# Down stage: operand sets and weights asked for product by product on one queue; the second norm between up products; another order of the tail

## The chip, the cores and the metric

The kernel runs on one core of one Trainium2 chip. The metric is the device time of one execution in microseconds; a kernel is run several times and the median is compared. The core has five engines that each work through their own list of instructions in order: TensorE (PE; its weight loads are listed as PEld), VectorE (DVE), ScalarE (ACT), GpSimd (POOL) and SyncE (SP). They wait for each other by semaphores. DMA transfers are asked for by an instruction on one engine's list and then run beside the engines.

## The reference

The reference is one layer of a decoder trunk, applied to a prompt of 512 tokens and to 8 sequences of 4 new tokens, in float32, with D = 2048 and D_FF = 5504. What matters here is its second half:

```python
    h = h + jnp.concatenate([o_gla, o_nsa], axis=-1) @ w_out[i]
    f, conv_new = conv_ffn(rmsnorm(h, ffn_norm_g[i]), conv_s[i], ffn_w_up[i], ffn_conv_w[i],
                           ffn_conv_b[i], ffn_w_down[i])
    h = h + f
    h = h + jax.nn.sigmoid(h @ ple_w_gate[i] + ple_b_gate[i]) * (p[i] @ ple_w_proj[i])
...
y = rmsnorm(h, final_norm_g)
...
def conv_ffn(xn, prefix, w_up, conv_w, conv_b, w_down):
    a, u = jnp.split(xn @ w_up, 2, axis=-1)
    a_all = jnp.concatenate([prefix.astype(a.dtype), a], axis=1)
    c = a_all[:, 0:L] * conv_w[0] + a_all[:, 1:L + 1] * conv_w[1] + a_all[:, 2:L + 2] * conv_w[2] + conv_b
    h = jax.nn.gelu(c) * u
    return h @ w_down, a_all[:, -(CONV_W - 1):]
```

The outputs are y for both groups of tokens, the new cache rows, the new states, and the convolution's last rows.

## The kernel before

All 544 tokens stand along the free dimension, as two groups (G) of 272 columns (256 of the prompt, 16 new). Every operand of a product is split into a high part h, rounded to fp32r by ACT, and a low part l, the rest, formed by VectorE (`split`, lines L919 and L920; with a scale L1104 and L1105); a product of two numbers is h·h + h·l + l·h, so each 128 x 128 block of weights costs three matmuls. Weights come from memory by SP into a tile raw and are split into wh (ACT) and wl (VectorE).

The stages that matter, in order:

1. **w_out** (`half_out`): 16 blocks of rows, two PSUM banks (mp, mq). VectorE adds each into the residual (L1003); scaled residuals are split at once into the operands of up (a11, s1, s2, a12, s3). ACT squares each residual and VectorE adds it to acc2 (L1127). At the end `rms_bcast` turns acc2 into R2, one factor for each token: ones times acc2 on TensorE (L209, into the bank ob), a chain of small VectorE steps that end in rs_y (L211 to L216), a broadcast over the partitions on TensorE (L220, L222) and copies into R2 (L223 on ACT, L224 on VectorE). Since the norm is a factor of each token, up works on operands without it and applies R2 to its results (ae, L1242, and gl, L1258).
2. **Up**: 43 columns in the order `UP_ORDER`. Each column takes seven products (Strassen-Winograd) in place of eight: X with a11, Y with s1, X with s2, Z with a12, X with s3, Y with s4, X with a22, with 24 matmuls each (L1185). Weights are combined on VectorE between them (raw<-raw). The first two columns run together, product by product, so that the operands of s4 and a22 (`late_operands`) can be made meanwhile. A column ends with the convolution and the gelu, which leave one hidden tile uu; POOL stores the convolution's rows (cvo, L1246 to L1248). After every second column `pair_operands` forms the seven operands of the down stage, and SP stores them in memory (dd_a.., dd_s.., L1271; those of the last column, L1277).
3. **Down**: three phases over the hidden dimension (`PHASES`), each with four pairs of columns that run together (`together`); a column here yields two blocks of 128 outputs for each group. Again seven products a column, of 21 matmuls (24 for some in the last phase). The seven operand sets of a phase, da11, ds1, ds2, da12, ds3, ds4 and da22, are read back from memory in two pieces each by POOL's queue (L1324) into a staging tile sg, of which there are three, and split from there into h and l. The sets of the next phase replace those of the old one while the phase's last pair runs (`refill`). The results of a column are gathered in two tiles e (three buffers each) and added to the residual in memory by POOL's queue (rd<-e, L1367).
4. **Gates**: 16 blocks, each a full product, a sigmoid, and a multiplication by the projected input embedding (L1413 to L1422), with squares gathered in acc3.
5. **Tail**: the last two gates go group by group. After the second of them for one group `rms_bcast` makes R3 for that group, and every residual is multiplied by it (L1443), shared between VectorE and POOL by `YSEQ`, and stored by SP (L1444), two rows of blocks at a time.

The code is written in program order; a scheduler then sets the order of each engine's list from its own estimates, and `tc.issue_after(x)` forces an instruction behind x. Tiles come from pools, and a tile in a used place waits until its last reader is done.

## Time and profile before

| what | value |
|---|---|
| median of three runs | 2736.88 us (2735.01 to 2738.28) |
| the profiled execution | 2739.89 us |
| its span, first to last instruction | 2738.1 us |
| mean granted clock of TensorE | 0.986 |
| busy share of the span | PE 97%, PEld 95%, DVE 65%, ACT 42%, POOL 17% |

The profile is that of one execution. Its time contains the span and some 2 us around it. The granted clock is the share of TensorE's full speed (2.4 GHz) that it was given; 0.50 is the lower of its two levels. A row of a timeline gives start, length and what is computed from what; a number in brackets is the time for which the engine stood still before that instruction, with what released it. A length contains the overlap with the next instruction, so a series of equal instructions is better counted by their starts.

### The profile page before, as it was taken

The numbers are of one execution on the slowest core, as the hardware profiler recorded it, in microseconds if no ns is written. First come the engines' busy times: TensorE is split into PE (matmuls) and PEld (weight loads), VectorE is DVE, ScalarE is ACT, GpSimd is POOL, SyncE is SP. The second block draws the span as 40 slices with busy tenths as digits, with TensorE's granted clock in tenths as the row PEclk, the third lists the DMA queues.
The fourth block names the chain that finished last, engine by engine and source line by source line (L and its number), as shares of the span: only waits on it lengthen the run. The fifth ranks groups of instructions, "written<-read, shape, count | busy, mean of one in ns | idle before, by whom it ended". The sixth has DMA issues, their size and how long they took to land.

```text
span 2738.1 us, 51117 instructions
## 1 busy us (share of the span) xinstructions
PE 2654.1 (97%) x21258; PEld 2604.7 (95%) x21258; DVE 1776.0 (65%) x2545; ACT 1151.6 (42%) x1811; POOL 458.7 (17%) x617
## 2 busy tenths in 40 slices
PE   8999999999999999899999999999979999999996
PEld 7999999999999789899999999999979999999996
DVE  5323543322256677898888888888878777866434
ACT  4333433221135455454445444544445544544332
POOL 4531101101201200121112111211121111102001
PEclk9999999999999999999999999999989999999998
DMA  6432222332524824333433443334337565646332
GB/s 245 134 108 72 93 95 94 111 106 90 204 70 160 306 82 135 113 123 122 141 121 111 132 134 118 120 120 142 122 129 203 172 166 140 209 120 185 117 110 85
DMA packets 130217, 366.88 MB, mean 134 GB/s; under 512 B 16928, under 2 KB 42512, under 8 KB 126912
## 3 DMA queue, kind: packets, MB, share of 16 engines
q1 hardware_dynamic: 101840, 280.42, 31.0%
q0 software_dynamic: 28144, 83.18, 10.9%
q8 instruction: 167, 2.74, 0.4%
q14 instruction: 66, 0.54, 0.1%
HBM read 298.93 MB, written 64.61 MB: 133 GB/s over the span
## 4 chain that ended last, share of the span: by engine, by line
PE 80%; issue 8%; DMA 3%; DVE 2%; POOL 1%; ACT 1%; SPq 0%; DVEq 0%; POOLq 0%; ACTq 0%
PE mp L178 27%; PE X L1185 25%; PE Y L1185 12%; PE Z L1185 6%; PE mq L178 3%; PE sp L359 2%; DMA sg<-dd_a 1%; PE sp L996 1%; DMA KV<-in_cache_slc,idx 1%; POOL KV L338 1%; DMA sg<-dd_s 1%; PE so L616 0%; PE sp L956 0%; DVE resid L1443 0%; POOL rd L1367 0%
## 5 line engine op out<-in xcount | busy, mean ns | idle before, releaser
L919 ACT CAST wh<-raw 128x1024 fp32r<-128x1024 f32 (+1 forms) x397 | 405.3, 1031 | 487.6 <-PE X L1185 227.0
L920 DVE TENSOR_TENSOR wl<-raw,wh 128x1024 fp32r<-128x1024 f32 (+1 forms) x397 | 471.4, 1196 | 85.1 <-ACT wh L919 85.0
L168 ACT CAST wh<-raw 128x1024 fp32r<-128x1024 f32 (+2 forms) x175 | 171.9, 985 | 456.9 <-PE mp L178 405.8
L169 DVE TENSOR_TENSOR wl<-raw,wh 128x1024 fp32r<-128x1024 f32 (+2 forms) x175 | 200.0, 1145 | 221.2 <-ACT wh L168 217.4
L178 PE MATMUL mp<-xh,wh 128*128 128x272 f32 x1408 | 297.4, 291 | 2.5 <-DVE qk L465 2.5
L178 PE MATMUL mp<-xl,wh 128*128 128x272 f32 x1408 | 299.6, 292 | 0.0
L178 PE MATMUL mp<-xh,wl 128*128 128x272 f32 x1408 | 297.2, 292 | 0.8 <-DVE wl L169 0.8
L178 PEld LDWEIGHTS mp<-xh,wh 128*128 128x128 f32 x1408 | 223.5, 190 | 4.7 <-issue 2.7
L178 PEld LDWEIGHTS mp<-xl,wh 128*128 128x128 f32 x1408 | 223.8, 190 | 1.9 <-issue 0.7
L178 PEld LDWEIGHTS mp<-xh,wl 128*128 128x128 f32 x1408 | 223.4, 190 | 2.2 <-DVE wl L169 1.1
L1246 POOL COPY cvo<-ae 128x2 f32<-128x2 f32 x43 | 54.1, 1259 | 715.6 <-DVE ae L1242 715.6
L1185 PE MATMUL Y<-s,wh 128*128 128x272 f32 x688 | 131.8, 287 | 0.0
L1185 PE MATMUL X<-a,wh 128*128 128x272 f32 x688 | 131.2, 288 | 0.0
L1104 ACT ACTIVATE wh<-raw 128x896 fp32r<-128x896 f32 (+1 forms) x72 | 69.4, 965 | 99.3 <-PE X L1185 43.8
L1185 PEld LDWEIGHTS X<-a,wh 128*128 128x128 f32 x688 | 108.4, 189 | 0.0
L1185 PEld LDWEIGHTS Y<-s,wh 128*128 128x128 f32 x688 | 107.8, 188 | 0.0
L1105 DVE SCALAR_TENSOR_TENSOR wl<-raw,wh 128x896 fp32r<-128x896 f32 (+1 forms) x72 | 79.4, 1105 | 32.5 <-ACT wh L1104 32.4
L1185 PE MATMUL Z<-a12h,wh 128*128 128x272 f32 x344 | 99.9, 290 | 0.0
L1185 PE MATMUL X<-a11h,wh 128*128 128x272 f32 x344 | 99.9, 290 | 0.0
L1185 PE MATMUL X<-s2h,wh 128*128 128x272 f32 x344 | 99.6, 290 | 0.0
L1185 PE MATMUL X<-a11l,wh 128*128 128x272 f32 x344 | 99.5, 289 | 0.0
L1185 PE MATMUL X<-s3h,wh 128*128 128x272 f32 x344 | 99.4, 289 | 0.0
(524 smaller groups left out, 8078.3 us busy)
## 6 DMA issues: line engine op xcount, KB each, us to landing
raw<-in_w_up SPq DMA_DIRECT2D x172, 512.0 KB, 4.6
raw<-in_w_in SPq DMA_DIRECT2D x89, 512.0 KB, 3.6
raw<-in_w_db SPq DMA_DIRECT2D x48, 448.0 KB, 4.1
raw<-in_w_gate SPq DMA_DIRECT2D x32, 512.0 KB, 3.5
raw<-in_w_da SPq DMA_DIRECT2D x32, 448.0 KB, 3.9
rd<-e POOLq DMA_DIRECT2D x48, 272.0 KB, 4.5
raw<-in_w_out SPq DMA_DIRECT2D x24, 512.0 KB, 3.6
dd_s<-st SPq DMA_DIRECT2D x65, 136.0 KB, 5.0
```

The source lines that it names most:

```text
L168: nc.scalar.copy(wh[:, :m], raw[:, s:s + m])
L169: nc.vector.tensor_sub(wl[:, :m], raw[:, s:s + m], wh[:, :m].bitcast(F32))
L178: mm = nc.tensor.matmul(pp[g][:, :GN] if isinstance(pp, list) else pp[:, g, :GN], w, x[:, g], start=first, stop=last)
L338: nc.gpsimd.indirect_dma_start(out=out, out_offset=None, in_=I[cache], in_offset=bass.IndirectOffsetOnAxis(ap=idx[:, 4 * b + pg:4 * b + pg ...
L359: nc.tensor.matmul(at[j // 16], w1[j // 16][:, j % 16], rows[:, :, j % 16], start=j == 0, stop=j == 31, skip_group_check=True)
L919: nc.scalar.copy(hi, src)
L920: nc.vector.tensor_sub(lo, src, hi.bitcast(F32))
L996: nc.tensor.matmul(so, V[:, c, g * 128:g * 128 + 128], PT[:, c * 128:c * 128 + 128], start=False, stop=i == 1 and c == qt)
L1104: nc.scalar.activation(hl[0], src, AF.Copy, scale=scale)
L1105: nc.vector.scalar_tensor_tensor(hl[1], src, scale, hl[0].bitcast(F32), op0=ALU.mult, op1=ALU.subtract)
L1185: nc.tensor.matmul(ps[:, :GN], w[wi][:, k], a[k][xi], start=start and k == 0 and i == 0, stop=stop and k == n - 1 and i == 2, skip_group_c ...
L1246: nc.gpsimd.tensor_copy(cvo[:, 0:2], ae[:, 512:514])
```

## The change

The change has five parts, and the lists of instructions before and after show where each one lands.

**The norm of up.** `rms_bcast` becomes a generator (`rms_steps`) with a stop after the small VectorE chain and one after the broadcast. It no longer stands between w_out and up, but is one more member of `together` for the first two columns. The bank ob gets a pool of its own ahead of X, Y and Z, kept until the end of down; uu has three buffers in place of four.

TensorE's list at the end of w_out, before (onh and onl are the operands of w_out, mq its bank):

```order
L178 MATMUL mq<-onl_9384,wh 128x272 x2
L178 MATMUL mq<-onh_9383,wl 128x272 x2
L209 MATMUL ob<-ones,acc_10771 128x1 x5
L220 MATMUL ob<-cn,rs_y 128x128 x4
L222 MATMUL ob<-cn,rs_y 128x32
L1185 MATMUL X<-a11h_10688,wh 128x272
L1185 MATMUL X<-a11l_10689,wh 128x272
```

After, 24 rows of X<-a11 of the first column follow w_out's last row; this is where they end:

```order
L1193 MATMUL X<-a11l_10703,wh 128x272
L1193 MATMUL X<-a11h_10702,wl 128x272
L213 MATMUL ob<-ones,acc_10771 128x1 x5
L1193 MATMUL X<-a11h_10688,wh 128x272
L1193 MATMUL X<-a11l_10689,wh 128x272
L1193 MATMUL Y<-s1h_10704,wh 128x272
```

and, some 200 rows later, inside X<-s3:

```order
L1193 MATMUL X<-s3h_10762,wh 128x272
L1193 MATMUL X<-s3l_10763,wh 128x272
L225 MATMUL ob<-cn,rs_y 128x128 x4
L227 MATMUL ob<-cn,rs_y 128x32
L1193 MATMUL X<-s3h_10762,wl 128x272
L1193 MATMUL X<-s3h_10764,wh 128x272
```

The column sums (ob<-ones,acc) have moved behind the first column's X<-a11, and the broadcast (ob<-cn,rs_y) into X<-s3.

**The opening of down.** For the first pair of columns, sets and weights are asked for in the order of the products, all on SP's queue, each forced behind the one before (`in_order`): da11, a weight block for each of the two columns, ds1, two weight blocks, and so on. The staging tile sg is gone for all phases: a piece is loaded straight into the place of its l part, ACT rounds it into h, and VectorE replaces it by the difference.

SP's list at the end of up, before (raw<-in_w_da and raw<-in_w_db are weights of down):

```order
L1271 DMA dd_s_11749<-st 128x272
L1198 DMA raw<-in_w_da 128x896
L1271 DMA dd_s_11758<-st 128x272
L1198 DMA raw<-in_w_da 128x896
L1198 DMA raw<-in_w_db 128x896 x3
L1277 DMA dd_a_11743<-uu 128x272
L1277 DMA dd_s_11746<-uu 128x272
```

and after:

```order
L1279 DMA dd_s_11726<-st 128x272
L1279 DMA dd_s_11735<-st 128x272
L1360 DMA da11l<-dd_a_11718 128x1088
L1358 DMA da11l<-dd_a_11718 128x816
L1358 DMA raw<-in_w_da 128x896 x2
L1358 DMA ds1l<-dd_s_11721 128x1088
L1358 DMA ds1l<-dd_s_11721 128x816
L1358 DMA raw<-in_w_da 128x896 x2
L1358 DMA ds2l<-dd_s_11724 128x1088
L1358 DMA ds2l<-dd_s_11724 128x816
```

The loads of the sets, which stood on POOL's list behind the last out_conv, now stand on SP's, with the weights between them; the stores of the last column (L1277, now L1285) follow behind all of them.

VectorE's list at the first wl of Z, before (ds1l to da12l are l parts of sets; the last row is that wl, of the first column):

```order
L1105 SCALAR_TENSOR_TENSOR ds2l<-sg,ds2h 128x1088
L920 TENSOR_TENSOR wl<-raw,wh 128x896
L1105 SCALAR_TENSOR_TENSOR ds2l<-sg,ds2h 128x816
L1345 TENSOR_TENSOR raw<-raw 128x896
L920 TENSOR_TENSOR wl<-raw,wh 128x896
L920 TENSOR_TENSOR da12l<-sg,da12h 128x1088
L920 TENSOR_TENSOR wl<-raw,wh 128x896
L920 TENSOR_TENSOR da12l<-sg,da12h 128x816
L1105 SCALAR_TENSOR_TENSOR wl<-raw,wh 128x896
```

and after:

```order
L1283 TENSOR_TENSOR st<-uu 128x272
L1414 TENSOR_TENSOR raw<-raw 128x896
L1400 TENSOR_TENSOR raw<-raw 128x896
L926 TENSOR_TENSOR da12l<-da12l,da12h 128x1088
L926 TENSOR_TENSOR da12l<-da12l,da12h 128x816
L1400 TENSOR_TENSOR raw<-raw 128x896
L926 TENSOR_TENSOR wl<-raw,wh 128x896
L926 TENSOR_TENSOR ds3l<-ds3l,ds3h 128x1088
L926 TENSOR_TENSOR ds3l<-ds3l,ds3h 128x816
L926 TENSOR_TENSOR wl<-raw,wh 128x896
L1112 SCALAR_TENSOR_TENSOR wl<-raw,wh 128x896
```

Both pieces of ds3l, which followed that wl before, now stand ahead of the first wl of Z (the last row), and so do more of the additions raw<-raw. Ahead of these rows stand da11l, ds1l, ds2l and, of the last up column, ae, cc, gl and uu.

**Refills.** At a switch of phase the load of a set is still on POOL's list, but its target is the l part itself, so it waits until the set's last product is done. ACT's list at the first switch, before (e<-X and e<-Y are the copies of finished products of the new pair; wh in the order of the products X, X, Y, Y):

```order
L1365 COPY e_23770<-X 128x272
L919 CAST ds4h<-sg 128x816
L1365 COPY e_23809<-X 128x272
L919 CAST wh<-raw 128x896
L1337 COPY e_24242<-X 128x272
L919 CAST da22h<-sg 128x1088
L1337 COPY e_24281<-X 128x272
L919 CAST da22h<-sg 128x816
L919 CAST wh<-raw 128x896
L1342 COPY e_24243<-Y 128x272
```

and after:

```order
L1386 COPY e_24222<-X 128x272
L925 CAST ds4h<-ds4l 128x816
L925 CAST wh<-raw 128x896
L1386 COPY e_24261<-X 128x272
L925 CAST da22h<-da22l 128x1088
L925 CAST wh<-raw 128x896
L925 CAST da22h<-da22l 128x816
L1394 COPY e_24223<-Y 128x272
L1394 COPY e_24262<-Y 128x272
```

Before, both pieces of da22h and the copy of the second column's X stand ahead of the second wh of Y; after, that wh stands ahead of them.

**Gate.** Each bank of the gates is taken when its weights are, with nothing else of it changed.

**Tail.** POOL multiplies nothing any more; VectorE multiplies both halves of a pair in one instruction of 2 x 272 columns. The first group's broadcast stands 24 matmuls before the last one, six of the first group's pairs are multiplied before the last gate is finished and two behind it, then follow the second group's eight. In between, the last gate's sgt, resid and acc stand behind the sixth of them.

The diff, cut to its core:

```diff
-    def product(pp, ws, xs, groups=slice(0, G)):
+    def product(pp, ws, xs, groups=slice(0, G), ks=None):
         n = len(ws)
-        for k, ((wh, wl), (xh, xl)) in enumerate(zip(ws, xs)):
+        for k in ks or range(n):
+            (wh, wl), (xh, xl) = ws[k], xs[k]
...
-    def rms_bcast(pl, fa, n, fo, psum):
+    def rms_bcast(*args):
+        for done in rms_steps(*args):
+            pass
+        return done
+
+    def rms_steps(pl, fa, n, fo, psum):
...
+        yield
         pp = psum()
         pq = pp[:, 128 * full:w] if w <= 512 else psum()[:, :rest]
         for i in range(full):
             nc.tensor.matmul(pp[:, i * 128:i * 128 + 128], y[:, i:i + 1].broadcast_to([128, 128]), ident,
                              start=True, stop=True)
-        nc.tensor.matmul(pq, y[:, full:full + 1].broadcast_to([128, 128]), ident[:, 128 - rest:], start=True, stop=True)
+        mm = nc.tensor.matmul(pq, y[:, full:full + 1].broadcast_to([128, 128]), ident[:, 128 - rest:], start=True, stop=True)
+        yield mm
         nc.scalar.copy(fo[:, :128 * full], pp[:, :128 * full])
-        return nc.vector.tensor_copy(fo[:, 128 * full:], pq)
+        yield nc.vector.tensor_copy(fo[:, 128 * full:], pq)
...
-    ac, ac_s = pool("acc", "right")
-    acc = ac.tile([128, G, GN], F32, name="acc2")
+    aq, aq_s = pool("acc", "right")
+    acc = aq.tile([128, G, GN], F32, name="acc2")
+    ac, ac_s = pool("sqs", "right")
...
-    rms_bcast(ac, flat(acc), D, flat(R2), one_bank)
     ac_s.close()
     mq_s.close()
     mp_s.close()
     more.clear()
+    ob, ob_s = psum_pool("ob")
+    more.append(ob)
     wf, wf_s = pool("wf", "left")
     fp, fp_s = pool("ffn", "left")
...
+    def norm():
+        yield
+        yield
+        steps = rms_steps(aq, flat(acc), D, flat(R2), one_bank)
+        for _ in steps:
+            yield
+
     def together(gens):
         while gens:
-            gens = [g for g in gens if next(g, gens) is None]
+            gens = [g for g in gens if next(g, gens) is not gens]
...
+        hids.append(fp.tile([128, G, GN], F32, tag="uu", bufs=3, name="uu"))
         if i == 1:
-            together([up(UP_ORDER[j], late, hids[j]) for j in range(2)])
+            together([up(UP_ORDER[j], late, hids[j]) for j in range(2)] + [norm()])
...
+
+    assert nraw[0] % 8 >= 3
+    for _ in range(nraw[0] % 8 - 3):
+        wf.tile([128, 8, 128], F32, tag="raw", bufs=5, name="skip")
     dp, dp_s = pool("down", "left")
     D_ = {}
 
-    def load_set(name, ph):
+    def load_set(name, ph, load=nc.gpsimd.dma_start):
         n = set_size(name, ph)
         pl = dl if name in ("s4", "a22") else dr
         hl = [pl.tile([128, PK + 1, GN], F32R, tag=name + c, bufs=1, name=f"d{name}{c}") for c in "hl"]
         for j in range(0, n, 4):
             m = min(4, n - j)
-            t = dp.tile([128, 4, GN], F32, tag="sg", bufs=3, name="sg")
-            nc.gpsimd.dma_start(t[:, :m], ddram[name, ph][:, j:j + m])
+            t = hl[1][:, j:j + m].bitcast(F32)
+            load(t, ddram[name, ph][:, j:j + m])
             f = lambda a: a.rearrange("p k n -> p (k n)")
-            split_scaled([f(a[:, j:j + m]) for a in hl], f(t[:, :m]), -1.0 if name == "s2" else None)
+            split_scaled([f(a[:, j:j + m]) for a in hl], f(t), -1.0 if name == "s2" else None)
         D_[name] = [[a[:, j] for a in hl] for j in range(n)]
 
+    def nothing(name):
+        pass
+
+    queued = []
+
+    def in_order(out, src):
+
+        if queued:
+            with tc.issue_after(queued[-1].ins):
+                queued.append(nc.sync.dma_start(out, src))
+        else:
+            queued.append(nc.sync.dma_start(out, src))
+
+    def opening(name):
+        if name not in D_:
+            load_set(name, 0, in_order)
+
     def down(n, ph, after):
-        r11, r12, r22, r21 = [next_raw(I["w_d%s%d" % ("ab"[u], ph)][2 * n + j], PK + (u == 0 and ph == PHASES - 1))
-                              for j, u in ((0, 0), (1, 0), (1, 1), (0, 1))]
+
+        opens = ph == 0 and n < 2
+        before = opening if opens else nothing
+        load = in_order if opens else nc.sync.dma_start
+
+        def weight(j, u):
+            return next_raw(I["w_d%s%d" % ("ab"[u], ph)][2 * n + j], PK + (u == 0 and ph == PHASES - 1), load)
+
+        order = ((0, 0), (1, 0), (1, 1), (0, 1))
+        if not opens:
+            r11, r12, r22, r21 = [weight(j, u) for j, u in order]
+        before("a11")
+        if opens:
+            r11 = weight(*order[0])
         ka, kb = set_size("a11", ph), PK
...
+        before("s1")
+        if opens:
+            r12 = weight(*order[1])
...
+        before("a12")
+        if opens:
+            r21 = weight(*order[3])
+        before("s3")
...
+        before("s4")
...
+        before("a22")
...
-    def nothing(name):
-        pass
-
-    for name in DSETS:
-        load_set(name, 0)
...
-    def gate(n, ws, pp, pj, p):
-        product(pp, ws, xn, p)
+    def gate(n, pp, pj, p):
...
+    def leave(g, n0, n1):
+        for n in range(n0, n1):
+            y2 = rpair[n][:, :, g]
+            nc.vector.tensor_mul(y2, y2, R3[:, g].unsqueeze(1).broadcast_to([128, 2, GN]))
+            nc.sync.dma_start(O["yT"][2 * n:2 * n + 2, :, g].rearrange("n p t -> p n t"), y2)
...
+        pp = main_ps()
         if n < KD - 2:
-            gate(n, ws, main_ps(), pj, every)
+            product(pp, ws, xn)
+            gate(n, pp, pj, every)
         else:
-            tail.append((n, ws, main_ps(), pj))
-    for g in range(G):
-        for a in tail:
-            gate(*a, slice(g, g + 1))
-        done = rms_bcast(yp, acc[:, g], D, R3[:, g], one_bank)
-    for g in range(G):
-        for n in range(KD // 2):
-            y2 = rpair[n][:, :, g]
-            e = nc.gpsimd if YSEQ[g][n] == "p" else nc.vector
-            with tc.issue_after(done.ins) if e is nc.vector and (g or n >= NTAIL) else ExitStack():
-                for i in range(2):
-                    e.tensor_mul(y2[:, i], y2[:, i], R3[:, g])
-            nc.sync.dma_start(O["yT"][2 * n:2 * n + 2, :, g].rearrange("n p t -> p n t"), y2)
+            tail.append((n, ws, pp, pj))
+
+    g0, g1 = slice(0, 1), slice(1, 2)
+    for n, ws, pp, pj in tail:
+        product(pp, ws, xn, g0)
+        gate(n, pp, pj, g0)
+    norm0, norm1 = [rms_steps(yp, acc[:, g], D, R3[:, g], one_bank) for g in range(G)]
+    (na, wa, pa, ja), (nb, wb, pb, jb) = tail
+    product(pa, wa, xn, g1, range(0, HK))
+    next(norm0)
+    product(pa, wa, xn, g1, range(HK, KD))
+    gate(na, pa, ja, g1)
+    product(pb, wb, xn, g1, range(0, HK))
+    spread = next(norm0)
+    next(norm0)
+    with tc.issue_after(spread.ins):
+        product(pb, wb, xn, g1, range(HK, KD))
+    leave(0, 0, 6)
+    done = gate(nb, pb, jb, g1)
+    with tc.issue_after(done.ins):
+        leave(0, 6, HK)
+    for _ in norm1:
+        pass
+    leave(1, 0, HK)
 
```

## Rows read from the trace of the kernel before

**Rows 1.** What TensorE (PE) waited for, by the view of waits, in three stretches: 1090 to 1130 us (w_out to up), 2020 to 2130 (up to down), 2160 to 2520 (both phase switches and the start of the gates). Columns: engine, tile and line that waited, what released it, us in total, times, longest.

```profile
PE ob L220 <- DVE rs_y L216: 6.7, 1, 6.7
PE ob L209 <- DVE acc L1127: 3.6, 1, 3.6
...
PE X L1185 <- ACT da11h L919: 14.5, 1, 14.5
...
PE Y L1185 <- ACT wh L919: 3.4, 2, 2.3
PE X L1185 <- ACT wh L919: 1.8, 2, 1.5
PE mp L178 <- ACT e L1365: 1.3, 1, 1.3
```

**Rows 2.** Busy time of each engine by stretches. Columns: stretch and its length, then busy us with the number of instructions for PE, PEld, DVE, ACT, POOL, then the granted clock (1.00 is 2.4 GHz, 0.50 is 1.2 GHz), the DMA share and GB/s.

```profile
1109.00:1117.30 8.30, 2.19 (x11) 2.19 (x11) 5.75 (x15) 0.08 (x1) 4.61 (x7) 0.50 0.17 56
...
1121.00:1125.00 4.00, 4.00 (x34) 4.00 (x33) 3.96 (x12) 3.31 (x9) 0.00 (x0) 1.00 0.00 0
...
2206.00:2211.00 5.00, 4.56 (x18) 4.24 (x19) 3.94 (x5) 2.15 (x4) 0.53 (x1) 0.50 0.43 149
...
2362.50:2366.00 3.50, 3.50 (x17) 3.50 (x18) 2.37 (x3) 0.14 (x1) 0.00 (x0) 0.55 0.00 0
```

**Rows 3.** Timeline of TensorE between w_out and up: start, length, engine and line, operation, out<-in, and in brackets the idle time before it with what ended it.

```profile
1102.33 0.41 PE L178 MATMUL mq<-onh,wl 128*128 128x272 f32 x2
1106.37 2.01 PE L209 MATMUL ob<-ones,acc 128*128 128x1 f32 x10 [3.63 <-DVE acc L1127]
1115.11 2.08 PE L220 MATMUL ob<-cn,rs_y 128*128 128x128 f32 x8 [6.73 <-DVE rs_y L216]
1117.27 0.57 PE L1185 MATMUL X<-a11h,wh 128*128 128x272 f32 x1
...
1118.09 0.43 PE L1185 MATMUL X<-a11h,wh 128*128 128x272 f32 x1
1118.32 0.43 PE L1185 MATMUL X<-a11l,wh 128*128 128x272 f32 x1
```

**Rows 4.** Busy time of each engine from the end of w_out to the end of the first column pair of up (columns as in group 2).

```profile
1102.70:1161.30 58.60, 48.24 (x359) 48.11 (x359) 48.06 (x85) 29.69 (x53) 6.54 (x10) 0.88 0.36 119
```

**Rows 5.** Timeline of VectorE at the end of w_out.

```profile
1105.60 0.72 DVE L1127 TENSOR_TENSOR acc<-acc,sq 128x544 f32<-128x544 f32 x1
1106.24 0.43 DVE L920 TENSOR_TENSOR s1l<-st,s1h 128x272 fp32r<-128x272 f32 x1
...
1107.29 2.35 DVE L920 TENSOR_TENSOR wl<-raw,wh 128x1024 fp32r<-128x1024 f32 x2
```

**Rows 6.** The opening of down: timelines of SP's queue, POOL's queue, ACT, VectorE and TensorE (the row of TensorE is the first matmul of the second column pair), and the DMA issues of 2013 to 2060 (KB each, median us from issue to landing).

```profile
2019.73 0.32 SPq L1271 DMA_DIRECT2D dd_s<-st  x1
...
2035.69 1.07 POOL L1324 DMA_DIRECT2D sg<-dd_a  x2 [0.23 <-issue]
...
2039.44 1.10 ACT L919 CAST da11h<-sg 128x1088 fp32r<-128x1088 f32 x1 [3.18 <-DMA sg<-dd_a]
...
2027.07 2.08 DVE L1340 TENSOR_TENSOR raw<-raw 128x896 f32<-128x896 f32 x2
...
2040.57 2.26 DVE L920 TENSOR_TENSOR da11l<-sg,da11h 128x1088 fp32r<-128x1088 f32 x2 [2.32 <-ACT da11h L919]
...
2084.53 0.29 PE L1185 MATMUL X<-da11h,wh 128*128 128x272 f32 x1
...
sg<-dd_a POOLq DMA_DIRECT2D x2, 544.0 KB, 4.0
```

**Rows 7.** The switches of phase: timeline of TensorE and of ACT at the first one (2203 to 2206 us), and the DMA issues of 2190 to 2215.

```profile
2203.43 0.29 PE L1185 MATMUL Y<-ds1l,wh 128*128 128x272 f32 x1
2203.55 0.29 PE L1185 MATMUL Y<-ds1h,wl 128*128 128x272 f32 x1
2206.14 0.59 PE L1185 MATMUL Y<-ds1h,wh 128*128 128x272 f32 x1 [2.30 <-ACT wh L919]
...
2203.52 0.39 ACT L1337 COPY e<-X 128x272 f32<-128x272 f32 x1 [2.70 <-DMA rd<-e]
...
sg<-dd_a POOLq DMA_DIRECT2D x3, 544.0 KB, 6.6
rd<-e POOLq DMA_DIRECT2D x4, 272.0 KB, 8.3
```

**Rows 8.** The tail: timeline of VectorE (L1414 is the last gate's sgt, L224 the copy of R of the second group, L1443 the final multiplications) and of POOL, busy time from 2729.4 to 2736.4, and the DMA traffic of 2720 to 2738.2, in 40 equal slices, with its issues.

```profile
2716.32 0.99 DVE L1414 TENSOR_TENSOR sgt<-sgt,pj 128x272 f32<-128x272 f32 x1
...
2724.45 0.17 DVE L224 COPY R<-ob 128x16 f32<-128x16 f32 x1 [2.02 <-ACT R L223]
2724.55 8.37 DVE L1443 TENSOR_TENSOR resid<-resid,R 128x272 f32<-128x272 f32 x14
...
2724.70 5.45 POOL L1443 TENSOR_TENSOR resid<-resid,R 128x272 f32<-128x272 f32 x6 [7.70 <-DVE R L224]
...
2729.40:2736.40 7.00, 0.00 (x0) 0.00 (x0) 3.51 (x9) 0.00 (x0) 0.76 (x1) 0.50 0.93 322
...
GB/s 0 0 0 0 0 0 0 0 0 0 0 0 0 0 12 323 278 0 10 304 347 366 203 340 268 62 349 349 383 344 373 359 347 378 359 352 19 0 0 0
out_yT<-resid SPq DMA_DIRECT2D x10, 272.0 KB, 2.6
```

More of the change, by code (lines that the diff above doesn't have):

```diff
@@ L1191, in trunk, with next_raw @@
     nraw = [0]
-    def next_raw(src, kn=8):
+    def next_raw(src, kn=8, load=nc.sync.dma_start):
         i = nraw[0] % 8
@@ L1197, in next_raw @@
         raw = pl.tile([128, 8, 128], F32, tag="raw", bufs=bufs, name="raw")
-        nc.sync.dma_start(raw[:, :kn], src)
+        load(raw[:, :kn], src)
         return raw
@@ L1344, in down @@
         yield
+        before("s2")
+        if opens:
+            r22 = weight(*order[2])
         nc.vector.tensor_sub(r11[:, :kb], r11[:, :kb], r22[:, :kb])
@@ L1385, in trunk @@
     st_s.close()
+    ob_s.close()
+    more.clear()
     if stop == "ffn":
@@ L1416, in gate @@
         if n == 0:
-            nc.scalar.activation(acc, r, AF.Square)
+            done = nc.scalar.activation(acc, r, AF.Square)
         else:
@@ L1420, in gate @@
             nc.scalar.activation(sq, r, AF.Square)
[L1421 removed]
+            done = nc.vector.tensor_add(acc[:, p], acc[:, p], sq)
         nc.scalar.activation(r, r, AF.Copy, scale=v1("yg", n))
+        return done
+    def leave(g, n0, n1):
[3 more added lines that the diff above has]
+            nc.sync.dma_start(O["yT"][2 * n:2 * n + 2, :, g].rearrange("n p t -> p n t"), y2)
     tail = []
```

6 lines of the change are left out of this document (2 added, 4 removed).

## Prediction

> **What bounds the kernel now.** TensorE is busy 97% of the span, so only a stretch in which TensorE stands still or runs at the low clock can give time back. I therefore read first what TensorE waited for in the stretches that the edits touch [rows 1], then the granted clock around those waits [rows 2], and then the engine that ends each wait. A matmul of 272 columns follows its forerunner after 0.125 us at the high level [rows 7] and after 0.227 us at the low one [rows 3]; so every matmul at the low clock (0.50 in rows 2) costs 0.10 us. Four seams lose time: between w_out and up, at the opening of down, at the two phase switches, and the tail, where after the last matmul VectorE and then the output transfers end last.
>
> **Norm between up products (seam 1).** Before, the last w_out matmul ends at 1102.7 and the first up product starts at 1117.27 [rows 3]: 14.5 us, of which 3.6 and 6.7 are waits [rows 1] and the rest is the norm's own matmuls at 0.50 clock; some 12 up matmuls more run slow (1.3 us). In all 15.8 us. After, 24 up matmuls (3.0 us) go first. What remains, worked through in the new order: acc2 is complete at 1106.3 [rows 5], so the sum over rows waits 0.6 and costs 1.2 (2.01 us for ten at the low clock, [rows 3], at the high one about half); the second column's first product needs a wl that VectorE finishes at 1108.5 (2.35 us for two from 1107.29, [rows 5]), 0.8 late; its second product needs a wl queued behind raw additions and operands of s4 and a22, about 1.7 late; 0.9 once more at the third; the broadcast 1.1. That is 6.3 left, so 9.5 back. Upper bound: VectorE is busy 48.06 of the 58.6 us to the end of this pair [rows 4], and its work is unchanged, so the pair can't end more than 10.5 us earlier. Lower: if a 1.7 us gap drops the clock (2 us) and the order costs another gap as long, 6. The later copy of R is wanted only where a column ends (ae), a pair of 336 matmuls on, and costs nothing; uu in three buffers instead of four costs nothing while a column's stores land before the third column after it writes uu, and without that cover the price is a wait of that column's first ACT copies.
>
> **Opening of down (seam 2).** Before, TensorE waits 14.5 us for da11h [rows 1] and more in pieces afterwards, with the clock down; the first load (sg) is issued at 2035.69 because on POOL's queue it stands behind the last column's copies and out_conv [rows 6]. After, da11l is asked for on SP right behind the dd_s store at 2019.73, so issued at about 2020.1; with the 4.0 us of such a load it has landed by about 2024.5, and ACT's cast (1.10) ends by 2025.6 [rows 6]. But then VectorE decides. In the new order 32 instructions stand on it from da11l to the first wl of Z: five sets at 2.12 (2.26 less the overlap, [rows 6]) are 10.6; 13 of 896 columns at 1.0 (2.08 for two) are 13; two cc, ae, gl and uu (512 to 560 columns) at the 0.64 of [rows 5] are 3.2; small ones 0.6: 27.4 us. So Z starts at about 2053.0. By then 84 of 294 matmuls are done; 210 remain at 0.125, 26.3 us, and some 2 us of low clock: the pair ends at 2081, before at 2084.5 [rows 6]. Gain 3.5. Bounds: the sets, weights and stores are about 10.3 MB, 30 us at the 340 GB/s of a full window (the windows of rows 8 show 322 to 366), so they land at about 2050; were the last one 6 us later, the pair would end later than now, at -3; and were VectorE's work fully covered, +8. The weights that are no longer asked for at 2013 to 2022 are in this sum (they stand between the sets on SP); the last column's stores, now behind all loads, are wanted only at the third phase, 300 us on. On ACT the copies of X out of PSUM stand behind da22h, the last set to land; X is wanted again about one product (2.6 us) after Z begins, so up to about 2055 that wait is covered and beyond it costs one for one. A rule speaks against this edit: the Trainium skill, "DMA: Bandwidth & Descriptors", section "Issuing engines are not separate DMA queues", says that all queues share the same 16 engines and that another issuing engine saves only sequencer time. By it the sum would be 3.5 us less; the trace shows that here sequencer time is the matter, since POOL issued its first load 16 us after that store.
>
> **Phase switches.** Before, ACT's copy of e waits for rd<-e (2.70 us at the first switch), because that transfer takes 8.3 us behind refills [rows 7]; the cast of the next wh stands behind it, and TensorE waits 5.2 us in four places [rows 1], then runs some 28 and 16 matmuls slow (4.4 us). Together about 10. After, the wh of both Y products stand ahead of that copy, so the same wait meets a later need: 5 to 8 us of slack. Against it, each refill now starts only when its set's last product has ended, instead of going ahead into sg. Its two halves take 4 to 6.6 us each to land [rows 6, 7], about 8 together; ACT, in order, waits for them with the casts of the products after it behind. Going through the pair at 2.6 us a product, each such wait ends within 0 to 2 us of the moment TensorE wants the next wh. I take 1.5 us lost at each switch: gain 7. Bounds: 10, nothing lost; -3, a low clock at both.
>
> **Gate and tail.** The first mp bank no longer waits for e: 1.3 [rows 1] back, less any wait for the weights, 0 to 1.4. In the tail the first group's multiplications start before the last matmul (its broadcast stands 24 matmuls earlier), and six of 0.64 (544 columns: 1105.60 to 1106.24, [rows 5]) from about 2709.0 end at 2712.9 instead of 2716.32 [rows 8]. The last sgt multiplication then takes 0.44 instead of 0.99, so R of the second group comes at 2720.6 instead of 2724.45 [rows 8]. Eight multiplications of 0.64 follow, all on VectorE; the eight transfers of 272 KB at about 355 GB/s [rows 8], 0.79 each, are the slower of the two: from 2722.9 to 2729.2, and the span ends 1.7 after the last traffic as now (2736.4 to 2738.1): 2730.6 to 2730.9. Gain 7.5. What carries this is that VectorE's multiplications (272 columns) are slow only beside POOL's: of the 14 that take 8.37 us in all, nine lie in a window with 0.76 us of POOL's work and take 3.51, 0.39 each, while the DMA engines are 93% busy; the five ahead of it, beside POOL's 5.45 us, take 0.97 each [rows 8]. So not DMA but POOL slows them. The Trainium skill, "SBUF — State Buffer", section "Who interferes with whom", names the reason: a VectorE instruction with two SBUF inputs and a GpSimd one that reads SBUF exclude each other. By that rule the eight cost 5.1 us, which the rows agree with.
>
> **Sum.** 9.5 + 3.5 + 7 + 1.3 + 7.5 = 28.8 us. The profiled run took 2739.89 us (span 2738.1); 2711.1 is left. That run was 3.0 us over the median of the three, so I forecast 2708.
>
> **Rivals.** *Switches give nothing back*: the landing times of refills (6.6, 8.3) speak for it, the slack of the new ACT order against it; 2715. *The tail keeps its pace*: if a pair multiplication took twice 0.97 even without POOL, eight would last 15.5 us from 2720.6, and the end would stay at 2738; 2716; the nine in 3.51 speak against it. *Opening fully covered*: if VectorE's instructions overlap better than I count and TensorE gets all 14.5 us back; 2697; the 27.4 us of queued work speak against it. *Opening bound by transfers*: the last set lands 6 us late; 2714. *Slower*: without sg each of the 14 refills is waited for in ACT's in-order queue, and the waits reach TensorE. Without the switches the other edits give 21.8 us; so from 1.6 us per set on the kernel is slower, and at 2.5 us per set (of 8 us landing, after 5 of slack) it takes 2737 - 21.8 + 35 = 2750. For it: 14 sets, each with two transfers; against it: set and product are 31 us apart and wh runs ahead. *That the change doesn't do what it says* I exclude by the order for what stands where; not for what it brings.
>
> **How the numbers follow.** Forecast, 2702 to 2713: 0.50. Switches nothing or tail at its pace: 0.20. Opening bound by transfers, alone or with poor switches (2714 to 2722): 0.14. Opening covered: 0.09. Slower rival: 0.07, of which 0.04 ends over the present time by 0.2% and 0.02 within it. A measurement of this kernel tells some 0.2% (5.5 us) from no change. Faster 0.93, same 0.03, slower 0.04. The range runs from 2697 (opening covered) to 2722 (poor switches and late transfers).
>
> **What would show it.** Right, if TensorE has no wait over 2 us between the last w_out matmul and the first up pair's end, this pair ends near 1151.5, the first down pair near 2081 with VectorE without a pause from 2025 to 2053, no wait over 1.5 us at either switch, and the output transfers end within 10 us of R. Wrong, if ACT shows waits for da..l or ds..l loads followed by TensorE waits for wh in the last pair of a phase, if Z's first matmul comes after 2056, or if VectorE's pair multiplications take over 1 us.

## The result, and the profile after

The changed kernel takes 2719.25 us (median of five runs, 2713.07 to 2723.27), the kernel before 2736.88 (five runs, 2735.01 to 2744.79): a ratio of 0.9931 [0.9909, 0.9952], 17.6 us saved by the medians. The sign held, and the time lies in the range of 2697 to 2722. The forecast of 2708 did not hold: the time lies above the 2702 to 2713 given for it, near the 2715 of the rival *Switches give nothing back*.

The profiled execution took 2723.27 us, with a span of 2721.4 us. To compare it with the one before, I cut both at the same matmuls, read from the timelines of TensorE (us, each from one profile; an undisturbed pair of down columns takes 37.1, in the third phase 40.1):

| stretch | before | after | change | forecast |
|---|---|---|---|---|
| last w_out matmul to last up matmul | 923.3 | 914.7 | -8.6 | -9.5 |
| from there to the end of the first down pair | 58.65 | 55.76 | -2.9 | -3.5 |
| the pairs on both sides of the two switches, above their undisturbed length | 10.4 | 10.7 | +0.3 | -7 |
| last down pair to the first gate | 41.54 | 40.08 | -1.5 | -1.3 |
| last gate matmul to the end | 26.8 | 19.0 | -7.8 | -7.5 |
| from the last w_out matmul to the end | 1635.5 | 1614.8 | -20.7 | -28.8 |

So 20.7 of 28.8 us came, and what is missing is the switches. The rest of the distance lies ahead of the change: the last w_out matmul ended 4.0 us later in this profile (1106.6 against 1102.6), in code that is the same in both. Times of the trace of after are therefore 4.0 us late against those of before.

What TensorE waited for, by the view of waits of after, in the stretches 1090 to 1165, 2010 to 2130 and 2130 to 2520 us (engine, tile and line; what released it; us in total, times, longest). It answers to [rows 1]:

```profile
PE X L1193 <- ACT wh L925: 1.2, 2, 0.7
PE ob L213 <- DVE acc L1134: 0.6, 1, 0.6
...
PE Z L1193 <- DVE wl L1112: 2.7, 1, 2.7
PE Y L1193 <- ACT wh L925: 2.6, 2, 1.5
PE Z L1193 <- ACT wh L1111: 2.6, 1, 2.6
PE X L1193 <- ACT wh L1111: 1.8, 2, 1.3
...
PE X L1193 <- ACT wh L925: 7.1, 4, 2.0
```

The waits of 3.6, 6.7 and 14.5 us are gone. In their place stand many short ones at the opening, for VectorE and ACT, and at the switches (last row) 7.1 us in four places, where 5.2 us stood. The low clock behind the waits costs less than before: 1.7 us at the first switch (granted 0.50 from 2184.5 to 2187) and none at the second (1.00), against 2.2 and 1.9. So the loss at the switches is as large as before in all. Four rows of TensorE's timeline of after show the first seam, as [rows 3] did:

```profile
1106.39 0.41 PE L177 MATMUL mq<-onh,wl 128*128 128x272 f32 x2
1106.64 0.29 PE L1193 MATMUL X<-a11h,wh 128*128 128x272 f32 x1
...
1110.44 1.28 PE L213 MATMUL ob<-ones,acc 128*128 128x1 f32 x10 [0.62 <-DVE acc L1134]
...
1140.78 1.06 PE L225 MATMUL ob<-cn,rs_y 128*128 128x128 f32 x8
```

Up's first product follows w_out without a gap, the sum over the rows waits 0.62 us, and the broadcast 30 us later waits for nothing.

The opening of down, in the view of busy time by stretches of after (columns as in [rows 2]), from the first da11l subtraction to the first wl of Z, and the row of TensorE that starts the second column pair:

```profile
2020.50:2048.00 27.50, 16.31 (x94) 14.54 (x93) 27.48 (x31) 19.54 (x24) 2.63 (x3) 0.86 0.91 355
...
2077.08 0.29 PE L1193 MATMUL X<-da11h,wh 128*128 128x272 f32 x1
```

VectorE is busy for 27.48 of 27.50 us with 31 instructions; the forecast counted 32 and 27.4 us. The first load of a set is issued at 2015.57, right behind the two dd_s stores ahead of it on SP's list (2013.73 to 2015.48), and not 16 us behind one as in [rows 6].

The first switch in the timeline of ACT of after:

```profile
2180.81 1.10 ACT L925 CAST da12h<-da12l 128x1088 fp32r<-128x1088 f32 x1 [4.44 <-DMA da12l<-dd_a]
2181.82 0.93 ACT L925 CAST wh<-raw 128x896 fp32r<-128x896 f32 x1
...
2199.18 0.39 ACT L1386 COPY e<-X 128x272 f32<-128x272 f32 x1 [1.12 <-DMA rd<-e]
2200.40 1.10 ACT L925 CAST da22h<-da22l 128x1088 fp32r<-128x1088 f32 x1 [0.83 <-DMA da22l<-dd_a]
2201.40 0.93 ACT L925 CAST wh<-raw 128x896 fp32r<-128x896 f32 x1
```

POOL issued that load of da12l at 2172.78, when Z's last matmul had released its target (in the timeline of POOL):

```profile
2172.78 1.06 POOL L1344 DMA_DIRECT2D da12l<-dd_a  x2 [4.25 <-PE Z L1193]
```

It landed 8.0 us later, and ACT stood still for the last 4.44 us of that. The next wh, whose weights had long been there, is behind it on ACT's list and ends at 2182.7. TensorE's timeline shows who waited:

```profile
2182.80 0.39 PE L1193 MATMUL X<-da22h,wh 128*128 128x272 f32 x1 [2.01 <-ACT wh L925]
...
2202.39 0.39 PE L1193 MATMUL X<-ds2h,wh 128*128 128x272 f32 x1 [1.93 <-ACT wh L925]
```

The tail in the timeline of VectorE of after (L1471 is the last gate's sgt, L230 the copy of R, L1485 the final multiplications, two of 272 columns in each):

```profile
2700.15 3.90 DVE L1485 TENSOR_TENSOR resid<-resid,R 128x544 f32<-128x544 f32 x6
2703.97 0.43 DVE L1471 TENSOR_TENSOR sgt<-sgt,pj 128x272 f32<-128x272 f32 x1
...
2711.46 0.17 DVE L230 COPY R<-ob 128x16 f32<-128x16 f32 x1 [2.02 <-ACT R L229]
2711.67 5.17 DVE L1485 TENSOR_TENSOR resid<-resid,R 128x544 f32<-128x544 f32 x8
```

Six take 3.90 and eight 5.17 us, 0.65 each, and the span ends 9.9 us after R of the second group, before 13.7 [rows 8].

### The profile page after: what moved, and what is told of

It is laid out like the page before. It is cut to its first block, busy times and chain, and to the rows that moved or that the text cites. A ratio compares the mean times of both kernels' runs of the same rounds, so it can differ in the third digit from the quotient of the medians.

```text
span 2721.4 us, 51097 instructions
## 1 busy us (share of the span) xinstructions
PE 2659.3 (98%) x21258; PEld 2606.8 (96%) x21258; DVE 1770.4 (65%) x2541; ACT 1150.4 (42%) x1811; POOL 446.1 (16%) x591
## 3 DMA queue, kind: packets, MB, share of 16 engines
q0 software_dynamic: 26576, 76.36, 10.2%
## 4 chain that ended last, share of the span: by engine, by line
PE 91%; DVE 3%; issue 3%; DMA 2%; ACT 1%; POOL 0%; SPq 0%; DVEq 0%; POOLq 0%; ACTq 0%
PE mp L177 31%; PE X L1193 26%; PE Y L1193 13%; PE Z L1193 7%; PE mq L177 3%; PE sp L365 3%; PE sp L1002 1%; PE sp L962 1%; DMA xf<-in_xT 1%; DMA ds4l<-dd_s 1%; PE sp L983 1%; PE so L622 1%; PE sp L998 0%; ACT wh L925 0%; PE sp L851 0%
## 5 line engine op out<-in xcount | busy, mean ns | idle before, releaser
L1428 POOL DMA_DIRECT2D rd<-e x48 | 41.7, 868 | 371.3 <-DVE e L1421 327.0
L1193 PE MATMUL Y<-s1h,wh 128*128 128x272 f32 x344 | 99.4, 289 | 0.1
```

The lines of the kernel that those rows point to most:

```text
L1193: nc.tensor.matmul(ps[:, :GN], w[wi][:, k], a[k][xi], start=start and k == 0 and i == 0, stop=stop and k == n - 1 and i == 2, skip_group_c ...
L1428: nc.gpsimd.dma_start(rdram[2 * n + j], e[j], accum_op=ALU.add)
```

## The experiments

The runs were made on three chips. One of them takes 2776.51 us for the kernel before (16 runs): in its four profiles w_out ends 36 to 41 us later, but the stretches behind it that an edit leaves alone have the same lengths to about 1 us. Each run's time is compared with the kernel before on its own chip; the stretches of the table above are compared across all. The loss at the switches is the exception. In kernels whose switches are those of before it is 10.4 (before), 9.1 (norm alone), 10.1 (gates and tail alone) and 7.3 us (place of ob); in those whose switches are those of after it is 10.7, 12.3 (the changed kernel once more) and 8.9 (opening without subtractions). So a difference of under some 3 us between two single profiles shows nothing there.

**The norm alone: the kernel before with the norm edit.** Its core, with ob in a pool of its own and three uu buffers:

```diff
-            together([up(UP_ORDER[j], late, hids[j]) for j in range(2)])
+            together([up(UP_ORDER[j], late, hids[j]) for j in range(2)] + [norm()])
```

> The kernel before with the norm's edit alone (column sums and broadcast between the first up products, uu in three buffers). From the profiles of before and after, the stretch from the end of w_out to the end of up became 8.6 us shorter. Theory: that is the norm's edit alone, so this kernel takes 2728.3 us, 8.6 less than before, with TensorE waits of 3 to 4 us in pieces between 1102 and 1165. Rival: the 4 us by which the profile of after was later already at the end of w_out, in code that the change doesn't touch, come with this edit; then only about 4.6 less, 2732.3, and the end of w_out again near 1106.6.

2769.74 us, ratio 0.9979 [0.9968, 0.9991], 6.8 us less. Up is 8.8 us shorter and the wait of the first gate is gone (1.45 us), but the opening of down is 3.1 us longer: in the timeline of POOL the first load into sg, which followed at once before, now waits for a store out of st:

```profile
2072.33 0.54 POOL L1341 DMA_DIRECT2D sg<-dd_a  x1 [5.40 <-DMA dd_s<-st]
```

In the changed kernel there is no sg, and this wait does not occur. That the edit moves the tiles (uu has one buffer less) and so gives sg another place in memory is argued from the allocation and not tried. The norm's own size is confirmed.

**Gates and tail alone: the kernel before with those two edits.** Its core:

```diff
-                for i in range(2):
-                    e.tensor_mul(y2[:, i], y2[:, i], R3[:, g])
+            nc.vector.tensor_mul(y2, y2, R3[:, g].unsqueeze(1).broadcast_to([128, 2, GN]))
```

> The kernel before with the edits of the gates and the tail alone. Theory: 7.8 us from the last matmul to the end (26.8 down to 19.0) and 1.4 at the first gate, so 9.2 less than before, 2727.7. Rival: part of the 7.8 came from the state in which the earlier edits left the output queue and POOL; then less than 7.

2768.5 us, ratio 0.9968 [0.9955, 0.9981], 8.0 us less. The tail is 18.9 us long instead of 26.8, all that was expected of it. The gate gives nothing: its first bank still waits, by the view of waits of this kernel, in 2520 to 2580 us:

```profile
PE mp L179 <- ACT e L1373: 1.3, 1, 1.3
```

So the order in which banks and weights are taken is not what removed this wait in the changed kernel.

**The place of ob: the kernel before with a pool for ob ahead of X, Y and Z, never used, kept to the end of down.** Its core:

```diff
+    ob, ob_s = psum_pool("ob")
+    more.append(ob)
+    one_bank()
+    one_bank()
     wf, wf_s = pool("wf", "left")
```

> The kernel before, with nothing but a pool of its own for the two ob banks ahead of X, Y and Z, kept until the end of down and unused there (the norm stays where it was). The first gate's wait of 1.3 us went in the kernel with the norm's edit alone and stayed in the kernel with the tail's edit alone. Theory: it is the place of the banks, so that the first gate's mp no longer lies in the bank of the last X; then from the last pair's start to the first gate it is 40.1 us here, not 41.5. Rival: the order of the lists that the scheduler made with the norm moved; then 41.5.

One execution: 2735.67 us, and 40.08 us from the last pair to the first gate, as after. Nothing is computed differently, only the banks lie elsewhere, and the wait for the copy into e is gone. This settles the 1.46 us: they belong to the pool for ob, which came with the norm's edit. (From the end of w_out to the end this execution is 4.7 us shorter than before; the rest of that is mostly its switches, 7.3 us against 10.4, which no part of the edit explains.)

**Staging for the refills: the changed kernel, with refills loaded into sg first, as before.** Its core:

```diff
+            else:
+                t = dp.tile([128, 4, GN], F32, tag="sg", bufs=3, name="sg")[:, :m]
+                nc.gpsimd.dma_start(t, ddram[name, ph][:, j:j + m])
```

> The kernel after, but the refills at the phase switches go through the staging tile sg again, as before; the opening keeps its direct loads. Theory: in after each refill can only be asked for when its set's last product is done, and ACT then waits 3.7 to 4.4 us for da12l with the next wh behind it. With sg back that wait goes, but the wait for rd<-e and its order return, so the losses at both switches are those of before (5.8 and 4.6 us) instead of those of after (6.0 and 4.7): 2719, the same as after. Rival: the new order of ACT by itself would have taken the switch loss away, and direct loading is what spoiled it; then some 7 us less than after, 2712.

2757.86 us, ratio 0.9925 [0.9896, 0.9953]. The switches lose 9.4 us, inside the 8.9 to 12.3 of the kernels without sg. So no cost of taking the staging away is shown, and the 7 us that are missing do not come back with it. TensorE still waits for wh, by the view of waits of this kernel, in 2150 to 2440 us:

```profile
PE X L1193 <- ACT wh L925: 2.1, 2, 1.5
PE Y L1193 <- ACT wh L925: 2.0, 2, 1.1
```

Only what ACT waits for is another thing: at the first switch da12h waits at most 0.82 us for its load, but the copy of e again waits 1.71 us for rd<-e, and a wh 3.18 us for an addition raw<-raw on VectorE.

**ACT behind the weights: the changed kernel, with ACT's rounding of each refilled set forced behind the wh of the products that come next (three products later).** Loads, buffers and the amount of work stay as they are; VectorE's subtraction of a set, which needs its rounding, moves behind with it. Its core:

```diff
+    def let_go(keep):
+        while len(held) > 2 * keep:
+            with tc.issue_after(cast[0].ins):
+                split_scaled(*held.pop(0))
```

> The kernel after, with each refilled set's rounding on ACT forced behind the wh of the product that follows three places later (for a11 behind the wh of Z, and so on; the last three sets behind wh of the next phase's first pair). Theory: the switch loss is the wait for landing loads in ACT's in-order list, with wh behind it; then the waits at the phase switches fall from 10.7 us to 2 at most and the kernel takes 2710 to 2711. Rival: the loss comes from the transfers themselves (weights late, all queues full); then weights or rd<-e are waited for instead and it stays within 3 us of after.

2750.09 us, ratio 0.9909 [0.9887, 0.9932]. The switches lose 4.4 us instead of 10.7. In the timeline of ACT of this kernel the rounding of da12h comes with no wait, and what is left is a copy that waits for rd<-e and a wh that waits for VectorE:

```profile
2214.23 1.87 ACT L925 CAST da12h<-da12l 128x1088 fp32r<-128x1088 f32 x2
...
2229.73 0.39 ACT L1398 COPY e<-X 128x272 f32<-128x272 f32 x1 [2.15 <-DMA rd<-e]
...
2231.11 0.95 ACT L925 CAST wh<-raw 128x896 fp32r<-128x896 f32 x1 [0.50 <-DVE raw L1412]
```

With the same transfers the switches lose 6.3 us less than in the changed kernel's own profile, and 4.5 less than in the best of the three, once no wh has to wait for them. At 4.4 us, more than the 2 expected, something else remained; the next runs look for it.

**The changed kernel once more, on the chip of the next runs.**

> The changed kernel once more, beside the others of this set on one chip. From the end of w_out to the end its profile took 1614.8 us, the kernel before 1635.5. Theory: the 20.7 us between them are what the change gives, and a profile here shows 1614 to 1616 again; the ratio to the kernel before is 0.992 to 0.9935. Rival: the end of w_out, which the edits don't touch but which stood 4 us later in the profile of after, moves with the change; then it stands later here too than in kernels without the norm's edit, and the ratio stays nearer to 1.

2719.6 us (2716.75 to 2727.93), ratio 0.9935 [0.9914, 0.9956], switches 12.3 us, the opening 55.41.

**Four e buffers: the kernel with ACT behind the weights, and a fourth buffer for each e, so that no copy waits for rd<-e.**

```diff
-        e = [dp.tile([128, G, GN], F32, tag=f"e{j}", bufs=3, name=f"e{j}") for j in range(2)]
+        e = [dp.tile([128, G, GN], F32, tag=f"e{j}", bufs=4, name=f"e{j}") for j in range(2)]
```

> The kernel with the rounding of refills forced behind later wh, and with four buffers instead of three for the result tiles e. In that kernel 4.4 us of TensorE's time were still lost at the switches, beside waits of ACT for rd<-e of 2.15 and 2.38 us. Theory: those waits hold the copies of X and Y and the next wh behind them; with a fourth buffer they are gone and the loss falls to 1.5 us or less, so the time falls by some 2.5 us against e4_behind (stretch from the end of w_out: 1608.0 to about 1605.5). Rival: the wh waits for raw<-raw on VectorE, which is late with the l parts; then the loss stays within 1 us.

2713.57 us, ratio 0.9907 [0.989, 0.9924]; the switches lose the same 4.4 us. The wait for rd<-e is gone and nothing came of it: the theory that it was the rest falls. The wh that waits for raw from VectorE (0.56 us at the first switch, 1.83 at the second) stays, which leaves VectorE's order.

**What bounds the opening: the changed kernel without VectorE's subtractions for ds3l, ds4l and da22l of the first phase.** This leaves out part of the computation: in that phase the low parts of these three sets are not the right ones. Otherwise the engines' work is the same. Its core:

```diff
+            if ph == 0 and name in ("s3", "s4", "a22"):
+                nc.scalar.copy(f(hl[0][:, j:j + m]), f(t))
```

> The changed kernel, in which the opening of down leaves out the subtractions on VectorE that make ds3l, ds4l and da22l (those l parts keep the loaded values). That takes 6.4 us of work from VectorE, 2.1 of them ahead of the first wl of Z, and leaves every transfer and every matmul. Theory: VectorE bounds the opening; then Z starts 2 us earlier and the first pair of down lasts 50 to 52 us instead of 55.8. Rival: the transfers or ACT bound it; then it stays at 55 to 56.

One execution: 2715.58 us, and 52.88 us to the end of the first pair instead of 55.4 to 55.8. In the timeline of TensorE of this kernel Z's first wl costs 0.76 us of waiting (2.71 in after), while its wh is waited for longer:

```profile
2041.62 0.39 PE L1193 MATMUL Z<-da12h,wh 128*128 128x272 f32 x1 [3.74 <-ACT wh L1111]
...
2042.90 0.59 PE L1193 MATMUL Z<-da12h,wl 128*128 128x272 f32 x1 [0.76 <-DVE wl L1112]
```

Less work on VectorE shortens the opening by about 2.7 us, so VectorE, not the transfers, sets its length; of the some 6.5 us taken off it only the 2.2 of ds3l stood ahead of Z's first wl, and about as much came back. (52.88 is a little over the 50 to 52 expected.) What holds Z then is its wh: on ACT's list a wh that waits 4.13 us for an addition raw<-raw stands ahead of it.

**VectorE's order in the opening: the kernel with four e buffers; the first column's ds3l and the additions for its product stand behind Z's wl, and ACT's rounding of ds4 and da22 behind the copies of X.** Its core on VectorE's side:

```diff
+        hold[0] = zlow[0] if opens else None
         before("s3")
-        nc.vector.tensor_sub(r12[:, :kb], r12[:, :kb], r22[:, :kb])
+        with tc.issue_after(hold[0].ins) if hold[0] else ExitStack():
+            nc.vector.tensor_sub(r12[:, :kb], r12[:, :kb], r22[:, :kb])
```

> The kernel e5_four, and in the opening VectorE's ds3l and the additions for X<-ds3 are forced behind the first wl of Z, and ACT's rounding of ds4 and da22 behind the copies of X. No work is added or left out. Theory: VectorE's list ahead of Z is 4.1 us shorter, so Z starts about 4 us earlier and the first pair of down ends 2 to 4 us earlier; together with the switches some 10 us less than after, ratio to the kernel before near 0.989. Rival: VectorE's work is only put off and the later products wait for it, with the first pair's end unchanged.

2710.41 us (2709.6 to 2711.55), ratio 0.9898 [0.9882, 0.9915]; 51.58 us to the end of the first pair, 4.0 less, with all of the work. How much of it is VectorE's order and how much ACT's was not tried apart. TensorE's timeline shows both first waits of Z shorter (2.60 and 2.71 us in after):

```profile
2039.61 0.39 PE L1200 MATMUL Z<-da12h,wh 128*128 128x272 f32 x1 [1.69 <-ACT wh L1115]
...
2040.73 0.40 PE L1200 MATMUL Z<-da12h,wl 128*128 128x272 f32 x1 [0.61 <-DVE wl L1116]
```

At the first switch, which this run leaves as it was (4.4 us lost at both; the text put on record for the next run gives 4.1), the timeline of VectorE shows the two pieces of the refilled ds4l ahead of the additions that the next wh waits for:

```profile
2187.95 1.28 DVE L930 TENSOR_TENSOR ds4l<-ds4l,ds4h 128x1088 fp32r<-128x1088 f32 x1
2189.15 1.08 DVE L1416 TENSOR_TENSOR raw<-raw 128x896 f32<-128x896 f32 x1
2190.15 1.00 DVE L930 TENSOR_TENSOR ds4l<-ds4l,ds4h 128x816 fp32r<-128x816 f32 x1
2191.07 1.08 DVE L1416 TENSOR_TENSOR raw<-raw 128x896 f32<-128x896 f32 x1
```

**The refills' splits one product later still: the run before, with ds3, ds4 and da22 of a refill split one product later, rounding and subtraction both.** Its core:

```diff
-            let_go({"a11": 2, "s1": 1}.get(name, 0))
+            let_go({"a11": 3, "s1": 2, "s2": 1}.get(name, 0))
```

> The kernel e7_order, with ds3, ds4 and da22 of a refill split one product later still at the phase switch (ds3 behind the wh of Y, ds4 behind that of X<-ds2, da22 behind that of Z). The switches of e7_order still lose 4.1 us: VectorE has ds3l and ds4l ahead of the additions raw<-raw that the wh of X<-ds2 needs. Theory: VectorE's order is what is left; then the loss falls below 1.5 us at both switches together and the stretch from the end of w_out to the end goes from 1605.1 to about 1602.5. Rival: the l parts are then late for their own products and the loss only moves to X<-ds3, Y<-ds4 or X<-da22; then it stays within 1 us.

2708.67 us (2706.65 to 2710.91) against 2737.71 on this chip, ratio 0.9887 [0.987, 0.9903]; the switches lose 2.2 us instead of 4.4, more than the 1.5 expected. By the view of waits from 2150 to 2440 us, little is left of the 7.1 us of the changed kernel:

```profile
PE X L1200 <- ACT wh L928: 1.2, 1, 1.2
PE X L1200 <- DVE wl L930: 0.4, 1, 0.4
```

From the end of w_out to the end this version takes 1603.4 us; the changed kernel takes 1614.8 and 1615.8, the kernel before 1635.5. It is the best of the study.

## Why the prediction was right, and where not

**The switches: the step that failed.** The prediction said: "Going through the pair at 2.6 us a product, each such wait ends within 0 to 2 us of the moment TensorE wants the next wh. I take 1.5 us lost at each switch: gain 7." The gain was nothing: 4.5 to 7.8 us were lost at a switch in the two profiles of the changed kernel, 10.7 and 12.3 in all, against 10.4 before. The landing time was forecast well (about 8 us; 8.0 for the first half of da12l, 8.8 for the second), and so, in the profile of after, was the size of one wait: its four long ones are 1.2 to 2.0 us. The sum was wrong. It counted one wait of 1.5 us for a switch, where two long ones came at each, 3.9 us at the first and 3.2 at the second, and it put the low clock behind them at nothing (1.7 us at the first). In the second profile one of them was also longer, 3.65 us.

Two things bring them about. Each refill now starts when its set's last product ends, so that ACT meets da12l 4.44 us before it has landed, with the wh of X<-da22 behind it; that is the first wait. And the slack claimed for the wait for rd<-e holds only for the two wh of Y: the wh of X<-ds2, the product after Y, still stands behind waits of 1.52 us for ds4l, 1.12 for rd<-e and 0.83 for da22l; that is the second. The prediction named this as a sign of being wrong (waits of ACT for sets, followed by waits for wh in the last pair of a phase), and it is the mechanism of its rival *Slower*, at a size that only cancels the gain and so gives the time of *Switches give nothing back*. With the splits of the sets forced behind the wh, 4.5 to 7.9 us of it came back with the same transfers; one product later still, 2.2 us are left. Direct loading in place of sg is not shown to cost anything by itself.

**The norm.** Forecast 9.5, measured 8.6 (8.8 alone). The bound of 10.5 from VectorE's work held: at the end of the pair, together with the next column's first product, which now partly runs ahead of the pair's last, 10.2 us were won. The next three products then gave back some 1.5 us, with waits of 0.42, 0.58 and 0.43 us for wl and wh, while VectorE was busy for all 13.80 us of 1152.2 to 1166. The term was too large by what is late next, which the sum did not follow past the pair. The sum over the rows waited 0.62 (forecast 0.6), and no wait in the pair was over 2 us.

**The opening.** Forecast 3.5, measured 2.9 and 3.2, by the mechanism forecast: 27.48 us of VectorE without a pause up to Z's wl. The transfers were done by then (the last sets land 10.4 us after their issue, at about 2045), so *Opening bound by transfers* fell. The rule of the Trainium skill weighed there ("DMA: Bandwidth & Descriptors", section "Issuing engines are not separate DMA queues") speaks of the time that it takes to initiate a transfer, and the prediction read more into it. What kept the first load back in the kernel before was not that time but the list it stood on, as the timeline of POOL of before shows:

```profile
2029.82 3.09 POOL L1246 COPY cvo<-ae 128x2 f32<-128x2 f32 x1 [20.79 <-DVE ae L1242]
```

POOL waited 20.79 us for ae, copied, and issued the load behind that. No run separates the change of engine from the other parts of this edit (the weights between the sets, no staging), so the 2.9 us belong to all of it. The order of the lists was no fixed bound either: 4 us more came from another order on VectorE and ACT.

**The gate.** The size was right (1.3 against 1.46), but by luck, since the reason was wrong. The prediction put it on banks that are taken with their weights; with that edit alone the wait of 1.3 us stayed, and it went when ob got its own pool in the kernel before, which changes nothing but the places of the banks.

**The tail.** Forecast 7.5, measured 7.8, step by step: the last sgt 0.43 us (0.44), eight multiplications in 5.17 (5.1), the end 9.9 us after R. *The tail keeps its pace* fell. The rule of the Trainium skill, "SBUF — State Buffer", section "Who interferes with whom", agrees: without POOL's reads a multiplication of 544 columns takes 0.65 us here, while beside them one of 272 took 0.97 [rows 8].

**The level.** The forecast took off 3.0 us, since the profiled run of before lay that far above its median. The profiled run of after lies 4.0 us above its own. On the chips other than the slow one the end of w_out moves between 1102.6 and 1106.6 us: 1102.6 and 1102.9 in two kernels without the norm's edit, 1102.8 to 1106.6 in six with it. A part of it goes with a wait of TensorE for ACT between 900 and 1000 us: 2.2 us in after and 2.1 in the last kernel (1105.7), with a granted clock of 0.93 there; 1.0 and 1.4 us, with 0.97, in the second profile of the changed kernel (1104.1) and in the kernel with another place of ob (1102.9); none to 0.8 us, with 1.00, in before and in three kernels with the change. So this wait comes and goes with and without the change; whether the change has part in the rest I can't say from two profiles without it.

## What to carry to other kernels

When a wait is removed from an engine that works in order, look at what else on its list can wait and who stands behind it: here the instructions that fed TensorE had their data for microseconds and stood behind a load that nobody yet needed. Here it helped to put work on late data behind the work that the bounding engine wants next, on ACT and on VectorE, while loads that start earlier (staging) gave nothing that showed. Count every such wait, and the low clock behind it, and not one wait for a seam. And follow a sum past the seam: work that a full engine puts off there is late at the next product. Where a term is read from one profile, see first how much it moves when the code there is the same: here by some 3 us at the switches.

## What was not expected of the hardware

The time from issue to landing of a load depended far more on its place in the burst than on its size. At the opening, pieces of 544 KB took (issues of 2010 to 2060 us; KB each, median us to landing)

```profile
da11l<-dd_a SPq DMA_DIRECT2D x1, 544.0 KB, 3.8
...
da12l<-dd_a SPq DMA_DIRECT2D x1, 544.0 KB, 9.3
ds3l<-dd_s SPq DMA_DIRECT2D x1, 544.0 KB, 10.2
ds4l<-dd_s SPq DMA_DIRECT2D x1, 544.0 KB, 10.4
```

with 355 GB/s moving. The first is as fast as the 4.0 us of such a load in the kernel before [rows 6]; the last one took 6.6 us more, by an estimate from these rows two thirds of its time spent behind the others. Pieces of 136 KB took from 1.8 us (dd_s<-st) to 8.8 (dd_s<-uu) in the same window.

And one chip of the three needed 1.4% more for the same kernel. Its profiles (four kernels with edits) have that time ahead of the end of w_out.
